# Attention scores, softmax and the turning of weights, one query block at a time instead of two

## The chip, the cores and the metric

The kernel runs on one core of a Trainium2 chip. The metric is the device time of one execution in microseconds (us). Engines are named as in the profile: PE (TensorE, matmuls and transposes), DVE (VectorE), ACT (ScalarE), POOL (GpSimd), SP (SyncE, which issues the weight loads).

## What is computed

A two-layer decoder trunk on 512 tokens of width 1024, all in float32: attention, gated MLP, short convolution, gated MLP. The change lies in the attention of the first layer. It has 16 heads of 64: eight forgetting heads (a softmax with a decay added to the scores) and eight stick-breaking heads.

```python
def forgetting_attention(q, k, v, log_f):      # heads 0..7, per block of 128 queries
    logits = einsum('bhqd,bhkd->bhqk', qi, k) * scale
    logits = logits + fi[..., :, None] - cum_f[:, :, None, :]
    logits = where(key_pos <= q_pos, logits, -inf)
    return einsum('bhqk,bhkd->bhqd', softmax(logits), v)

def stick_breaking_attention(q, k, v):         # heads 8..15
    z = einsum('bhqd,bhkd->bhqk', qi, k) * scale
    log_one_minus = where(key_pos < q_pos, log_sigmoid(-z), 0)
    later = reverse cumsum of log_one_minus over keys, without the own one
    w = where(key_pos < q_pos, exp(log_sigmoid(z) + later), 0)
    return einsum('bhqk,bhkd->bhqd', w, v)
```

Queries and keys are RMS-normed per head before. The heads' outputs go through one output projection and are added to the residual.

## The kernel before

Every float32 operand of a large matmul is split into two parts of fewer bits (hi and lo), and a product is three matmuls: hi by hi, hi by lo, lo by hi. Weights come by SP in pieces of 512 KB; ACT makes hi (L228) and DVE makes lo by a subtraction (L235), up to two pieces ahead.

Heads go in pairs p = 0..7 (0 to 3 forgetting, 4 to 7 stick-breaking), the two heads e of a pair on partitions 0 to 63 and 64 to 127. There are four blocks b of 128 queries; a "half" is two of them (0 and 1, or 2 and 3). For each pair and half:

- `logits(p, half)`, L537: the scores. Three matmuls per head and block (q hi by k hi, q hi by k lo, q lo by k hi; L552), a fourth for the decay of forgetting heads (L556), and a mask (L558). They contract over 64 rows, so the two heads of a pair lie side by side in the array. Each head and block has a PSUM bank "b" of its own, four per call, and there are four such banks. Forgetting heads then take the maximum on DVE (L569), the exponential on ACT (L571) and, later, the reciprocal and the scaling on DVE (L575, L576). Stick-breaking heads take two sigmoids on ACT (L582, L583), a backward product scan on DVE (L585) and a product on DVE (L586). The scores of block b reach over (b + 1) x 128 keys, at least 256.
- `turn(p, half)`, L591: the weights are transposed on PE (L604) into a bank "c" per head and block (there are two such banks), copied by ACT to hi (L606) and by DVE to lo (L609), which releases the bank. The tiles `pt` for them exist twice, for the two heads of one half. POOL zeroes the quarter that stays empty (L614).
- `weigh(p, half)`, L616: weights by values (L628, L629), 8 or 16 matmuls into a bank "a"; the two parts are added by ACT and DVE (L638, L639) and split (L316, L317).

Queries and keys come token-major from the input projection (`heads`), are normed per head there (a power on POOL at L313, then DVE at L510 and L513), and are transposed per pair by `turn_heads` (L530) with hi on ACT (L534) and lo on DVE (L535), two pairs at a time, into the same two banks "c".

What sets the order: the program is written with a planner's clock. `spend` advances it by an estimate for the PE work issued; `after(us, fn)` issues fn once the clock has passed; `fill(us)` issues work of the other kind for so many us: the input projections of the next head groups (L474 to L476, 256 columns) and, from the fourth pair on, half of the output projection (L250 to L252, L657). A tile scheduler then orders each engine's queue from it and may move instructions past each other. The main loop, u over 16 halves, issues `logits(u)`, FILL1, `weigh(u - 2)`, FILL1, `turn(u - 1)` (with FILL1 behind each of its two blocks) and FILL2 or, from u = 12, FILL3. When the fillers are used up, the rest of the output projection follows.

Of the kernel before, what the change touches and what calls it, by code (L numbers as in the profile page):

```python
# [25 lines left out]
P = 128  # L26
S = 512
# [12 lines left out]
SCALE, SHARES, LATER = 8.0, 1.5, 1.5  # L40
# [4 lines left out]
FILL1, FILL2, FILL3 = 1.0, 4.4, 2.6  # L45
# [3 lines left out]
def trunk(  # L49
# [21 lines left out]
    def f32(ap):  # L71
        return ap.bitcast(F32)
# [464 lines left out]
    def logits(p, half):  # L537
# [5 lines left out]
        both = [(b, e) for b in (2 * half, 2 * half + 1) for e in range(2)]  # L543
        ss = {be: bank("b") for be in both}

        def of(b, e):
            return slice(e * HD, (e + 1) * HD), slice(b * P, (b + 1) * P), slice(0, max((b + 1) * P, 256))

        for step, (ql, kl) in enumerate(((q_hi, k_hi), (q_hi, k_lo), (q_lo, k_hi))):
            for be in both:  # L550
                rows, tok, keys = of(*be)
                pe.matmul(ss[be][:, keys], ql[rows, tok], kl[rows, keys], start=step == 0, stop=False)  # L552
        if fox:
            for be in both:
                rows, tok, keys = of(*be)
                pe.matmul(ss[be][:, keys], dl[rows, p, tok], dr[rows, keys], start=False, stop=False)  # L556
        for be in both:
            pe.matmul(ss[be][:, of(*be)[1]], ident16, masks[0 if fox else 1], start=False, stop=True)  # L558
        spend((4 if fox else 3) * (0.4, 0.23)[half == 0] + 0.5)
        ws = {}  # L560
        tiles = [aw.tile([P, (3, 7)[half], P], F32, tag=f"w{half}", name=f"w{p}{half}{e}", bufs=2) for e in range(2)]
        for b, e in both:
            n = (b + 1) * P
            ws[b, e] = tiles[e].rearrange("p k c -> p (k c)")[:, (b % 2) * (n - P):][:, 0:n]
        if fox:
            tops, totals, invs = (
                {be: tiny.tile([P, 1], F32, tag=t, name=f"{t}{p}{be[0]}{be[1]}", bufs=8) for be in both} for t in ("top", "total", "inv"))
            for be in both:
                dve.reduce_max(tops[be], ss[be][:, 0:(be[0] + 1) * P], axis=AX.X, negate=True)  # L569
            for be in both:  # L570
                act.activation(ws[be], ss[be][:, 0:(be[0] + 1) * P], AF.Exp, bias=tops[be], accum_out=totals[be])  # L571

            def shares():
                for be in both:
                    dve.reciprocal(invs[be], totals[be])  # L575
                    dve.tensor_scalar(ws[be], ws[be], invs[be], None, op0=ALU.mult)  # L576
            after(SHARES, shares)
        else:
            for b, e in both:
                n, s, w = (b + 1) * P, ss[b, e], ws[b, e]  # L580
# [10 lines left out]
    def turn(p, half, ws):  # L591

        pts[p, half] = []
        for e in range(2):
            both = [aw.tile([P, NB, 256], F32R, tag=f"pt{i}", name=f"pt{p}{half}{e}{i}", bufs=PT) for i in range(2)]
            pts[p, half].append(both)
        for b in (2 * half, 2 * half + 1):
            n = (b + 1) * P
            at_ = slice((b % 2) * P, (b % 2 + 1) * P)
            srcs = []  # L600
            for e in range(2):
                t = bank("c")
                for k in range(b + 1):
                    pe.transpose(t[:, k * P:(k + 1) * P], ws[b, e][:, k * P:(k + 1) * P], ident)  # L604
                srcs.append(t[:, 0:n].rearrange("p (k q) -> p k q", q=P))
                act.activation(pts[p, half][e][0][:, 0:b + 1, at_], srcs[e], AF.Copy)  # L606
# [293 lines left out]
```

## Time and profile before

| | us |
|---|---|
| median of 3 runs | 1256.09 |
| lowest, highest | 1255.18, 1488.36 |
| the profiled execution | 1255.41 |
| span of its instructions | 1253.7 |

The profile lists, per engine, how long it was busy and what ended its idle time. Matmuls overlap in it: one of 256 columns shows 0.28 us, though the next starts 0.12 us later, so a busy PE need not be PE at its peak. The granted clock is 1.00 where PE runs at 2.4 GHz and 0.50 where it runs at 1.2. The attention stage with its loop lies between 72 and 306 us of the span; the two MLPs and the convolution follow.

### The profile page before, as it was taken

How to read it: one execution, taken by the hardware profiler on the slowest of the kernel's cores; microseconds unless marked ns; L12 is line 12 of the kernel's file. 1: busy time of each engine (PE TensorE's matmuls, PEld its weight loads, DVE VectorE, ACT ScalarE, POOL GpSimd, SP SyncE). 2: the span in 40 equal slices, each digit the busy share in tenths (PEclk: the TensorE clock that was granted, in tenths of full speed). 3: DMA queues.
4: the chain of work that ended last, by engine and by line, in shares of the span. 5: the costliest groups of instructions: out<-in, count | busy, mean ns of one | idle time of the engine just before them, and what ended most of it. 6: DMA issues, size and time to landing. Idle time of an engine off the chain costs nothing.

```text
span 1253.7 us, 15395 instructions
## 1 busy us (share of the span) xinstructions
PE 1212.9 (97%) x6133; PEld 1008.8 (80%) x6133; DVE 747.1 (60%) x1104; ACT 500.5 (40%) x815; POOL 49.6 (4%) x114
## 2 busy tenths in 40 slices
PE   7989999987999999999999999999999999999998
PEld 7978988766888888888888888888888888888886
DVE  4575677886676777765333455555667777772312
ACT  5454566554444344443222222233343444432120
POOL 3211111100000000000000000000000000000000
PEclk8998999997999999999999999999999999999999
DMA  5321221210323333333333323323233333332330
GB/s 157 93 61 34 69 62 40 68 51 18 100 85 101 95 91 101 88 93 93 93 93 97 101 85 100 99 87 100 85 101 96 89 101 89 96 101 84 104 115 34
DMA packets 175272, 108.15 MB, mean 86 GB/s; under 512 B 4604, under 2 KB 168492, under 8 KB 175200
## 3 DMA queue, kind: packets, MB, share of 16 engines
q1 hardware_dynamic: 174944, 107.01, 28.7%
q8 instruction: 48, 0.79, 0.3%
q0 software_dynamic: 256, 0.16, 0.1%
q14 instruction: 24, 0.20, 0.0%
HBM read 105.06 MB, written 2.10 MB: 85 GB/s over the span
## 4 chain that ended last, share of the span: by engine, by line
PE 87%; DVE 7%; ACT 3%; POOL 1%; DMA 1%; issue 1%; SPq 0%; DVEq 0%; ACTq 0%
PE psb L250 11%; PE psb L252 11%; PE psa L250 11%; PE psb L251 11%; PE psa L252 11%; PE psa L251 11%; PE psa L474 4%; PE psa L476 4%; PE psa L475 4%; PE psb L474 2%; PE psb L475 2%; PE psb L476 2%; DVE rest L585 2%; POOL qr L313 1%; PE psc L604 1%; PE psb L552 1%
## 5 line engine op out<-in xcount | busy, mean ns | idle before, releaser
L228 ACT ACTIVATE whi<-raw 128x1024 fp32r<-128x1024 f32 (+2 forms) x198 | 208.4, 1053 | 357.8 <-PE psb L251 131.1
L235 DVE TENSOR_TENSOR wlo<-raw,whi 128x1024 fp32r<-128x1024 f32 (+2 forms) x198 | 240.3, 1214 | 178.1 <-ACT whi L228 177.3
L250 PE MATMUL psb<-hs_hi,whi 128*128 128x512 f32 x480 | 189.9, 396 | 0.0
L252 PE MATMUL psb<-hs_hi,wlo 128*128 128x512 f32 x480 | 189.8, 395 | 0.0
L251 PE MATMUL psb<-hs_lo,whi 128*128 128x512 f32 x480 | 188.7, 393 | 0.0
L250 PE MATMUL psa<-hs_hi,whi 128*128 128x512 f32 x416 | 164.7, 396 | 0.0
L252 PE MATMUL psa<-hs_hi,wlo 128*128 128x512 f32 x416 | 164.2, 395 | 0.0
L251 PE MATMUL psa<-hs_lo,whi 128*128 128x512 f32 x416 | 163.9, 394 | 0.0
L324 DVE SCALAR_TENSOR_TENSOR u<-y,taps,u 128x510 f32<-128x510 f32 (+1 forms) x176 | 131.0, 747 | 3.0
L474 PE MATMUL psa<-whi,hs_hi 128*128 128x256 f32 (+1 forms) x384 | 114.0, 298 | 3.8 <-ACT sq L505 1.9
L476 PE MATMUL psa<-whi,hs_lo 128*128 128x256 f32 (+1 forms) x384 | 110.9, 289 | 0.0
L475 PE MATMUL psa<-wlo,hs_hi 128*128 128x256 f32 (+1 forms) x384 | 110.6, 288 | 0.0
L251 PEld LDWEIGHTS psb<-hs_lo,whi 128*128 128x128 f32 x480 | 90.1, 188 | 21.4
L252 PEld LDWEIGHTS psb<-hs_hi,wlo 128*128 128x128 f32 x480 | 90.1, 188 | 21.4
L250 PEld LDWEIGHTS psb<-hs_hi,whi 128*128 128x128 f32 x480 | 90.3, 188 | 20.3
L252 PEld LDWEIGHTS psa<-hs_hi,wlo 128*128 128x128 f32 x416 | 78.1, 188 | 18.6
L251 PEld LDWEIGHTS psa<-hs_lo,whi 128*128 128x128 f32 x416 | 78.1, 188 | 18.4
L250 PEld LDWEIGHTS psa<-hs_hi,whi 128*128 128x128 f32 x416 | 78.2, 188 | 18.0
L774 DVE TENSOR_TENSOR y<-psb,nrow_n 128x512 f32<-128x512 f32 x44 | 30.4, 691 | 83.9 <-PE psb L252 83.9
L474 PEld LDWEIGHTS psa<-whi,hs_hi 128*128 128x128 f32 x384 | 75.0, 196 | 5.0 <-ACT sq L505 2.2
L316 ACT ACTIVATE a<-u 128x512 fp32r<-128x512 f32 x44 | 27.8, 631 | 118.7 <-DVE u L779 118.7
L475 PEld LDWEIGHTS psa<-wlo,hs_hi 128*128 128x128 f32 x384 | 75.0, 195 | 0.0
(202 smaller groups left out, 1918.2 us busy)
## 6 DMA issues: line engine op xcount, KB each, us to landing
raw<-in_ffn_w_up SPq DMA_DIRECT2D x88, 512.0 KB, 3.8
raw<-in_ffn_w_down SPq DMA_DIRECT2D x30, 512.0 KB, 3.5
raw<-in_attn_w_in SPq DMA_DIRECT2D x24, 512.0 KB, 4.3
raw<-in_conv_w_in SPq DMA_DIRECT2D x24, 512.0 KB, 3.8
raw<-in_ffn_w_down SPq DMA_DIRECT2D x16, 448.0 KB, 3.6
raw<-in_attn_w_out SPq DMA_DIRECT2D x8, 512.0 KB, 3.4
raw<-in_conv_w_out SPq DMA_DIRECT2D x8, 512.0 KB, 4.0
x_tok<-in_x SPq DMA_DIRECT2D x4, 512.0 KB, 7.9
```

The costliest lines, as they stand in the source:

```text
L228: made = act.activation(hi[:, 0:nk * n], raw[:, 0:nk * n], AF.Copy)
L235: dve.tensor_tensor(lo[:, 0:nk * n], raw[:, 0:nk * n], f32(hi[:, 0:nk * n]), op=ALU.subtract)
L250: pe.matmul(acc, w[0], rhs[0], start=first, stop=False)
L251: pe.matmul(acc, w[0], rhs[1], start=False, stop=False)
L252: pe.matmul(acc, w[1], rhs[0], start=False, stop=last)
L316: act.activation(hi, src, AF.Copy)
L324: dve.scalar_tensor_tensor(dst[:, d:], src[:, 0:S - d], tap(j), dst[:, d:], op0=ALU.mult, op1=ALU.add)
L474: pe.matmul(acc, lhs[0], w[0], start=first, stop=False)
L475: pe.matmul(acc, lhs[0], w[1], start=False, stop=False)
L476: pe.matmul(acc, lhs[1], w[0], start=False, stop=last)
L585: dve.tensor_tensor_scan(back, back, back, 1.0, op0=ALU.mult, op1=ALU.bypass)
L774: dve.tensor_tensor(y, acc, norm.row, op=ALU.mult)
```

## The change

Scores, softmax and turning go by one query block instead of a half; weighing still goes by halves. The main loop runs over 32 blocks g: `logits(g)`, FILL1, `weigh` of the half of block g - 2 if that was the half's second, `turn(g - 1)`, FILL2 or FILL3. Each call of `logits` takes two banks "b" instead of four. The fillers' total stays nearly the same: 8.4 us per half before (FILL1 four times and FILL2) and 2 x (1.0 + 3.2) = 8.4 after; in the last two pairs 6.6 before and 2 x (1.0 + 2.0) = 6.0 after. The tiles for weights are four of 512 columns instead of two of 384 and two of 896; the small tiles for maxima and sums exist four times instead of eight; POOL's memsets are issued ahead of a half's first turn instead of behind its second. How queries and keys are made and kept token-major is not changed.

```diff
-SCALE, SHARES, LATER = 8.0, 1.5, 1.5
+SCALE, SHARES, LATER = 8.0, 1.0, 1.5
+WB = 4
-FILL1, FILL2, FILL3 = 1.0, 4.4, 2.6
+FILL1, FILL2, FILL3 = 1.0, 3.2, 2.0
...
-    def logits(p, half):
+    def logits(p, b):
...
-        both = [(b, e) for b in (2 * half, 2 * half + 1) for e in range(2)]
-        ss = {be: bank("b") for be in both}
+        n = (b + 1) * P
+        wide = max(n, 256)
+        tok = slice(b * P, n)
+        ss = [bank("b") for _ in range(2)]
         for step, (ql, kl) in enumerate(((q_hi, k_hi), (q_hi, k_lo), (q_lo, k_hi))):
-            for be in both:
-                rows, tok, keys = of(*be)
-                pe.matmul(ss[be][:, keys], ql[rows, tok], kl[rows, keys], start=step == 0, stop=False)
+            for e in range(2):
+                rows = slice(e * HD, (e + 1) * HD)
+                pe.matmul(ss[e][:, 0:wide], ql[rows, tok], kl[rows, 0:wide], start=step == 0, stop=False)
...
-        spend((4 if fox else 3) * (0.4, 0.23)[half == 0] + 0.5)
-        ws = {}
-        tiles = [aw.tile([P, (3, 7)[half], P], F32, tag=f"w{half}", name=f"w{p}{half}{e}", bufs=2) for e in range(2)]
+        spend((4 if fox else 3) * wide * 0.00044 + 0.12)
+        ws = [aw.tile([P, S], F32, tag="w", name=f"w{p}{b}{e}", bufs=WB)[:, 0:n] for e in range(2)]
...
-    def turn(p, half, ws):
+    def turn(p, b, ws):
+        half, n = b // 2, (b + 1) * P
+        if b % 2 == 0:
+            pts[p, half] = []
+            for e in range(2):
+                both = [aw.tile([P, NB, 256], F32R, tag=f"pt{i}", name=f"pt{p}{half}{e}{i}", bufs=PT) for i in range(2)]
+                for t in both:
+                    pool.memset(f32(t[:, 2 * half + 1, 0:P]), 0.0)
+                pts[p, half].append(both)
...
-            spend(0.22 * (b + 1))
-            fill(FILL1)
-        for both in pts[p, half]:
-            for t in both:
-                pool.memset(f32(t[:, 2 * half + 1, 0:P]), 0.0)
+        spend(0.22 * (b + 1))
...
-    for u in range(16 + 2):
-        p, half = divmod(u, 2)
-        if u < 16:
-            waiting[u] = logits(p, half)
-            if u % 4 == 3 and p < 7:
+    blocks = [(p, b) for p in range(8) for b in range(NB)]
+    for g in range(len(blocks) + 2):
+        if g < len(blocks):
+            p, b = blocks[g]
+            waiting[g] = logits(p, b)
+            if p % 2 and p < 7 and b == 3:
                 turn_heads(p + 1)
                 turn_heads(p + 2)
             fill(FILL1)
-        if u >= 2:
-            weigh(*divmod(u - 2, 2))
-            if u - 2 == 7:
+        if g >= 2 and blocks[g - 2][1] % 2:
+            p, b = blocks[g - 2]
+            weigh(p, b // 2)
+            if (p, b) == (3, 3):
                 fillers.append(output(0, residual))
-        if 1 <= u <= 16:
-            fill(FILL1)
-            turn(*divmod(u - 1, 2), waiting.pop(u - 1))
-            fill(FILL2 if u < 12 else FILL3)
+        if 1 <= g <= len(blocks):
+            turn(*blocks[g - 1], waiting.pop(g - 1))
+            fill(FILL2 if g < 24 else FILL3)
```

Line numbers after are one higher than before ahead of `logits` (L250 becomes L251) and lower from there on (L552 becomes L551, L585 becomes L578, L604 becomes L599, L609 becomes L604, L628 becomes L619).

On PE, the scores of the last pair's first half (blocks 0 and 1) before: four banks (psb_3490 to psb_3493) are filled step by step, and the scheduler has put fillers (L250 to L252, output projection) into the run.

```order
L552 MATMUL psb_3490<-qk_hi_3076,qk_hi_3085 128x256
L552 MATMUL psb_3491<-qk_hi_3076,qk_hi_3085 128x256
L552 MATMUL psb_3492<-qk_hi_3076,qk_hi_3085 128x256
L552 MATMUL psb_3493<-qk_hi_3076,qk_hi_3085 128x256
L552 MATMUL psb_3490<-qk_lo_3077,qk_hi_3085 128x256
L552 MATMUL psb_3491<-qk_lo_3077,qk_hi_3085 128x256
L552 MATMUL psb_3492<-qk_lo_3077,qk_hi_3085 128x256
L552 MATMUL psb_3493<-qk_lo_3077,qk_hi_3085 128x256
L552 MATMUL psb_3490<-qk_hi_3076,qk_lo_3086 128x256
L552 MATMUL psb_3491<-qk_hi_3076,qk_lo_3086 128x256
L250 MATMUL psa_3463<-o_hi_300,whi_3195 128x512
```

The same place after, block 0 of that pair: two banks (psb_3530, psb_3531), the row ahead of them a filler.

```order
L253 MATMUL psa_3516<-o_hi_300,wlo_3256 128x512
L551 MATMUL psb_3530<-qk_hi_3165,qk_hi_3174 128x256
L551 MATMUL psb_3531<-qk_hi_3165,qk_hi_3174 128x256
L551 MATMUL psb_3530<-qk_lo_3166,qk_hi_3174 128x256
L551 MATMUL psb_3531<-qk_lo_3166,qk_hi_3174 128x256
L551 MATMUL psb_3530<-qk_hi_3165,qk_lo_3175 128x256
L551 MATMUL psb_3531<-qk_hi_3165,qk_lo_3175 128x256
```

Where one run filled four banks, two runs now fill two each, with other PE work between them: counted over the program, 28 runs of score matmuls stand on PE before and 44 after.

On DVE, the end of the attention before: the scan and product of the last pair's block 3 (rest_3639, rest_3644, w_3627, w_3628), and behind them the subtractions of that pair's first half (pt_3674, pt_3676).

```order
L586 TENSOR_TENSOR w_3628<-w_3628,rest_3634 128x383
L585 SCALAR_TENSOR_TENSOR rest_3639<-rest_3639 128x511
L639 TENSOR_TENSOR o_3666<-psa_3649,o_3666 64x256
L586 TENSOR_TENSOR w_3627<-w_3627,rest_3639 128x511
L585 SCALAR_TENSOR_TENSOR rest_3644<-rest_3644 128x511
L639 TENSOR_TENSOR o_3666<-psa_3649,o_3666 64x256
L586 TENSOR_TENSOR w_3628<-w_3628,rest_3644 128x511
L317 TENSOR_TENSOR o_lo_2868<-o_3666,o_hi_2867 128x256
L609 TENSOR_TENSOR pt_3674<-psc_3677,pt_3673 128x128
L609 TENSOR_TENSOR pt_3676<-psc_3680,pt_3675 128x128
```

The same place after: a weight split (L236), the scans and products of block 3, and behind them the subtractions of block 2 (pt_3748, pt_3752).

```order
L236 TENSOR_TENSOR wlo_3808<-raw_3806,whi_3807 128x1024
L578 SCALAR_TENSOR_TENSOR rest_3721<-rest_3721 128x511
L578 SCALAR_TENSOR_TENSOR rest_3726<-rest_3726 128x511
L579 TENSOR_TENSOR w_3719<-w_3719,rest_3721 128x511
L579 TENSOR_TENSOR w_3720<-w_3720,rest_3726 128x511
L630 TENSOR_TENSOR o_3740<-psa_3731,o_3740 64x256
L604 TENSOR_TENSOR pt_3748<-psc_3755,pt_3747 128x3x128
L630 TENSOR_TENSOR o_3740<-psa_3731,o_3740 64x256
L604 TENSOR_TENSOR pt_3752<-psc_3760,pt_3751 128x3x128
```

Before, the subtractions of blocks 0 and 1 stand behind the scans and products of blocks 2 and 3; after, those of blocks 0 and 1 have moved ahead of the scans of block 3, and those of block 2 stand behind its scans and products.

On PE, the end of the attention before: two rows of the weighing of the pair before the last, the turns of the last pair's block 0 (one transpose per head) and block 1 (two per head), and the next weighing.

```order
L628 MATMUL psa_3649<-pt_3560,v_2974 128x256
L629 MATMUL psa_3649<-pt_3561,v_2974 128x256
L604 MATMUL psc_3677<-ident,w_3511 128x128
L604 MATMUL psc_3680<-ident,w_3512 128x128
L604 MATMUL psc_3685<-ident,w_3511 128x128 x2
L604 MATMUL psc_3689<-ident,w_3512 128x128 x2
L628 MATMUL psa_3699<-pt_3673,v_2974 128x256
```

After, the end of the last pair's first weighing, then the turns of block 2 (three transposes per head) and block 3 (four), and the last weighing.

```order
L619 MATMUL psa_3731<-pt_3644,v_3036 128x256
L620 MATMUL psa_3731<-pt_3645,v_3036 128x256
L599 MATMUL psc_3755<-ident,w_3677 128x128 x3
L599 MATMUL psc_3760<-ident,w_3678 128x128 x3
L599 MATMUL psc_3767<-ident,w_3719 128x128 x4
L599 MATMUL psc_3773<-ident,w_3720 128x128 x4
L619 MATMUL psa_3781<-pt_3747,v_3036 128x256
```

In both, two turns stand one behind the other on PE with nothing between them, the second in the same two banks "c" as the first; before these are blocks 0 and 1 (and further back 2 and 3), after only blocks 2 and 3.

## Rows read from the trace of the kernel before

**Rows 1.** The page's head and its section 1: busy time and share of the span.
```profile
span 1253.7 us, 15395 instructions
PE 1212.9 (97%) x6133; PEld 1008.8 (80%) x6133; DVE 747.1 (60%) x1104; ACT 500.5 (40%) x815; POOL 49.6 (4%) x114
```

**Rows 2.** Stretches: us, busy PE, PEld, DVE, ACT, POOL, granted clock, DMA share, GB/s.
```profile
91.10:97.90 6.80, 5.79 (x27) 5.79 (x28) 3.65 (x12) 3.20 (x8) 0.00 (x0) 0.50 0.00 0
115.00:118.30 3.30, 3.30 (x17) 3.22 (x17) 1.71 (x3) 0.69 (x1) 0.35 (x2) 0.50 0.00 0
289.10:302.60 13.50, 8.42 (x32) 6.92 (x33) 8.86 (x18) 5.67 (x14) 0.82 (x4) 0.50 0.00 0
72.00:306.00 234.00, 207.46 (x1561) 185.75 (x1560) 172.31 (x368) 132.41 (x329) 28.69 (x66) 0.95 0.17 50
185.00:306.00 121.00, 103.36 (x720) 88.88 (x718) 92.70 (x170) 69.13 (x164) 12.30 (x38) 0.94 0.17 53
```

**Rows 3.** Waits of PE, 72 to 306 us: us in total, times, longest.
```profile
PE psc L604 <- DVE pt L609: 9.1, 5, 6.7
PE psc L530 <- DVE qk_lo L535: 4.8, 3, 2.0
PE psa L250 <- DVE o L639: 2.9, 2, 1.8
PE psb L552 <- ACT w L571: 1.9, 2, 1.5
PE psa L474 <- ACT sq L505: 1.9, 1, 1.9
...
PE psb L552 <- ACT w L583: 0.9, 1, 0.9
...
PE psa L628 <- ACT sq L505: 0.5, 1, 0.5
```

**Rows 4.** Timeline of PE around a long score run: start us, us, instruction, count.
```profile
258.23 0.39 PE L251 MATMUL psa<-o_lo,whi 128*128 128x512 f32 x1
258.46 0.39 PE L252 MATMUL psa<-o_hi,wlo 128*128 128x512 f32 x1
258.77 0.68 PE L552 MATMUL psb<-qk_hi,qk_hi 64*128 64x384 f32 x4
...
260.20 0.40 PE L558 MATMUL psb<-mask,ident 128*128 128x128 bf16 x4
260.40 0.48 PE L250 MATMUL psa<-o_hi,whi 128*128 128x512 f32 x1
```

**Rows 5.** Timeline of PE around a short score run.
```profile
273.02 0.39 PE L252 MATMUL psa<-o_hi,wlo 128*128 128x512 f32 x1
273.33 0.39 PE L552 MATMUL psb<-qk_hi,qk_lo 64*128 64x256 f32 x2
273.65 0.40 PE L558 MATMUL psb<-mask,ident 128*128 128x128 bf16 x4
273.86 0.48 PE L250 MATMUL psa<-o_hi,whi 128*128 128x512 f32 x1
```

**Rows 6.** Timeline of PE, 89 to 93 us; in brackets the idle time before.
```profile
89.77 0.44 PE L552 MATMUL psb<-qk_hi,qk_hi 64*128 64x384 f32 x1 [1.49 <-ACT w L571]
92.11 0.58 PE L474 MATMUL psa<-whi,hs_hi 128*128 128x256 f32 x1 [1.91 <-ACT sq L505]
```

**Rows 7.** Waits of PE, 284 to 306 us.
```profile
PE psc L604 <- DVE pt L609: 7.4, 2, 6.7
```

**Rows 8.** Groups of DVE by line and shape, 74 to 305 us: busy, mean ns, idle before.
```profile
L235 DVE TENSOR_TENSOR wlo<-raw,whi 128x1024 fp32r<-128x1024 f32 x22 | 26.9, 1222 | 12.4 <-ACT whi L228 12.3
L585 DVE TENSOR_TENSOR_SCAN rest<-rest 128x511 f32<-128x511 f32 x8 | 9.6, 1211 | 0.0
L609 DVE TENSOR_TENSOR pt<-psc,pt 128x384 fp32r<-128x384 f32 x16 | 8.7, 553 | 0.8 <-ACT pt L606 0.6
L586 DVE TENSOR_TENSOR w<-w,rest 128x511 f32<-128x511 f32 x8 | 5.4, 682 | 0.2
```

More of the change, by code (lines that the diff above doesn't have):

```diff
@@ L553, in logits @@
         if fox:
[L554 to L558, printed above, removed]
-        spend((4 if fox else 3) * (0.4, 0.23)[half == 0] + 0.5)
-        ws = {}
-        tiles = [aw.tile([P, (3, 7)[half], P], F32, tag=f"w{half}", name=f"w{p}{half}{e}", bufs=2) for e in range(2)]
@@ L562, in logits @@
-        for b, e in both:
-            n = (b + 1) * P
-            ws[b, e] = tiles[e].rearrange("p k c -> p (k c)")[:, (b % 2) * (n - P):][:, 0:n]
-        if fox:
[L566 to L571, printed above, removed]
+            for e in range(2):
+                rows = slice(e * HD, (e + 1) * HD)
+                pe.matmul(ss[e][:, 0:wide], dl[rows, p, tok], dr[rows, 0:wide], start=False, stop=False)
@@ new lines, in logits @@
+        for e in range(2):
+            pe.matmul(ss[e][:, tok], ident16, masks[0 if fox else 1], start=False, stop=True)
+        spend((4 if fox else 3) * wide * 0.00044 + 0.12)
+        ws = [aw.tile([P, S], F32, tag="w", name=f"w{p}{b}{e}", bufs=WB)[:, 0:n] for e in range(2)]
+        if fox:
+            tops, totals, invs = ([tiny.tile([P, 1], F32, tag=t, name=f"{t}{p}{b}{e}") for e in range(2)] for t in ("top", "total", "inv"))
+            for e in range(2):
+                dve.reduce_max(tops[e], ss[e][:, 0:n], axis=AX.X, negate=True)
+            for e in range(2):
+                act.activation(ws[e], ss[e][:, 0:n], AF.Exp, bias=tops[e], accum_out=totals[e])
@@ L573, in shares @@
             def shares():
-                for be in both:
-                    dve.reciprocal(invs[be], totals[be])
-                    dve.tensor_scalar(ws[be], ws[be], invs[be], None, op0=ALU.mult)
+                for e in range(2):
+                    dve.reciprocal(invs[e], totals[e])
+                    dve.tensor_scalar(ws[e], ws[e], invs[e], None, op0=ALU.mult)
             after(SHARES, shares)
         else:
-            for b, e in both:
-                n, s, w = (b + 1) * P, ss[b, e], ws[b, e]
+            for s, w, e in zip(ss, ws, range(2)):
```

29 lines of the change are left out of this document (11 added, 18 removed).

## The prediction

> **What bounds the kernel now.** The page comes first: TensorE (PE) is busy for 97% of the span, VectorE (DVE) for 60% [rows 1]. That share is an average over stages, so the table of stretches comes next. Outside the attention stage PE runs without a gap; the stage that the change touches is the stretch from 72 to 306 us, where PE is busy for 207.5 of 234 us at a mean granted clock of 0.95 [rows 2]. Third, the waits of PE in that stretch: eleven rows, 26.0 us in all, the largest for DVE's subtraction that finishes the turned weights, 9.1 us, of which one wait alone is 6.7 [rows 3]. Three pieces of the stretch ran at half the granted clock, that is at 1.2 instead of 2.4 GHz: 5.8, 3.3 and 8.4 us of PE work stood in them [rows 2]; at full clock that work takes half, so they cost (5.8 + 3.3 + 8.4) / 2 = 8.8 us. Waits and clock together are 34.8 us. That is the most that a better order of this stage can give: neither kernel issues more or fewer instructions than the other (6121 matmuls, 1106 DVE and 781 ScalarE instructions in both orders), with the same shapes, and the DMA queue's order is the same.
>
> DVE is the second thing to see. From 185 to 306 us, mostly the stick-breaking heads, it is busy for 92.7 of 121 us while PE is busy for 103.4 [rows 2]. The two take turns waiting for each other there; neither is full.
>
> The sums below are made against the profiled execution, 1255.4 us with a span of 1253.7. The median of the runs shown is 1256.1, so a forecast is 0.7 us higher against it; I leave that out.
>
> **Term 1, more runs of score matmuls: +6.1 us.** The score matmuls use 64 rows of the array, everything around them 128. A run of 16 of them (12 of 64 rows, 4 masks) stands between the matmuls at 258.46 and 260.40. Matmuls of 512 columns follow each other at 0.23 us (258.23, 258.46), so the run took 1.94 - 0.23 = 1.71 us [rows 4]. Its columns at 2.4 GHz, with the two heads of a pair side by side, are three times (384 + 512) and four masks of 128: 3200 / 2.4 = 1.33 us. The rest, 0.38 us, is paid at the run's ends. A short run of 6 took 0.84 - 0.23 = 0.61 us for 768 columns, 0.32 us: rest 0.29 [rows 5]. So the price hangs on the run and hardly on its length. In PE's order there are 28 such runs before and 44 after (some are cut by the scheduler in both). 16 x 0.38 = 6.1 us. Bounds: 16 x 0.29 = 4.6, and 16 x 0.61 = 9.8 if each new run cost as much as a whole short one. Nothing hides this, since it is PE's own time.
>
> The Trainium skill, page TensorEngine Tiling (Array Packing), section Tiling Modes (Key Properties), says that changing the tiling mode, and not just the tile, drains TensorE. By that rule the sum counts mode changes, which gives the 6.1 us above; if instead the 0.3 to 0.4 us belonged to the matmuls themselves, whose number does not change, this term would be nothing and the forecast 6 us lower. Two runs of very different length with nearly the same rest speak for the rule.
>
> **Term 2, scores waiting for their banks: -5 us.** A call of logits takes all four "b" banks before and two after, so the next block's scores no longer need the exponentials of the block just issued to be done. The waits that this removes are 1.9 (for L571) and 0.9 us (for L583) [rows 3]. The first stands at 89.77 as 1.49 us, with a wait of 1.91 us for ScalarE right behind it at 92.11 [rows 6]: 3.4 us in which PE did almost nothing, and then the clock was at half for 6.8 us, worth 5.8 / 2 = 2.9 us [rows 2]. In all 1.9 + 0.9 + 1.9 + 2.9 = 7.6; I take 5, since ScalarE's square in that chain still sits in the same queue. Bounds 0 and -7.6.
>
> **Term 3, turned weights, except the last: -1.7 us.** Two turns of one call stood FILL1 = 1.0 us apart, and the second needs the two "c" banks that DVE's subtraction of the first releases. Now FILL2 = 3.2, a call of logits and FILL1 stand between them, over 5 us. Of the 9.1 us [rows 3] 7.4 are in the tail [rows 7]; the other 1.7 goes. Bounds 0 and -1.7.
>
> **Term 4, turning queries and keys: -2 us.** PE waits 4.8 us in three places for DVE (L535) [rows 3]. In the new order eight of these transposes stand directly behind a run that fills two score banks; before, four stood behind a run that filled four. So DVE has half the maxima and scalings ahead of them. I take 2 of the 4.8, and no change of the short stretch at half clock at 115 us [rows 2]. Bounds +2 and -4.8.
>
> **Term 5, output and value matmuls waiting: -3 us.** The other waits, from 2.9 for DVE (L639) down to 0.5 [rows 3], come from DVE's queue: in it four scans and four products stand as one block of work, two and two now. The six waits of this sort (all eleven but L604, L530, the two of L552 and the square of term 2) are 26.0 - 9.1 - 4.8 - 2.8 - 1.9 = 7.4 us; I take 3. Bounds 0 and -7.4.
>
> **Term 6, the tail: -1.1 us.** At the end of the stage the fillers are used up, and one of PE's two waits for DVE there is 6.7 us [rows 7]. The new order has the same knot: the last turn (four transposes per head) needs the "c" banks of block 2, and in DVE's queue the subtractions that release them stand behind a weight split and both scans and both products of block 3. With DVE's times that is 1.22 + 2 x 1.21 + 2 x 0.68 + 0.55 = 5.6 us [rows 8]. 6.7 - 5.6 = 1.1 less; the stretch at half clock that goes with it stays. Bounds 0 and -6.7, the latter if PE's own work covered it, plus 4.2 us of clock (8.4 / 2).
>
> The moved memsets cost nothing: ScalarE waits in both orders for the memset of the round before, and PE's next weighing comes 5 us later. SP's queue is not moved.
>
> **Sum.** 6.1 - 5 - 1.7 - 2 - 3 - 1.1 = -6.7, and 1255.4 - 6.7 = 1248.7, say 1249 us. That is 0.5%, inside the 2% (25 us) that a measurement of this kernel can tell from no change.
>
> **Rivals.**
> *The waits dissolve.* With smaller blocks PE and DVE overlap and the pieces at half clock go with the gaps. For it: DVE was free for 28 us of the 121 [rows 2], so there is room. Against it: the order of the tail keeps its knot. All of it would be 6.1 - 34.8 = -28.7, 1227 us; with the tail left (7.4 and 4.2 us of clock) it is -17.1, 1238. I give the middle of it, 1233.
> *The waits only move.* The work is the same, PE waits for DVE in other places, and the 16 runs are what is left: 1255.4 + 6.1 = 1261.5. For it: DVE's total is unchanged and near PE's.
> *The weights of a stick-breaking block come too late (slower).* Between the scores of block 3 and its turn the planner now puts FILL1, weighing (0.88), a turn (0.66), FILL2 or FILL3, the next scores (0.46) and FILL1: 7.2 us, and in the last two head pairs 6.0. Before, FILL1 six times and FILL2 stood there, 10.4 us, with a weighing or two, a turn and the next scores besides. DVE needs 2 x (1.21 + 0.68) for the block, and ahead of it 1.22 for a weight split and 2 x 0.55 for the turned block before, 6.1 us [rows 8], without ScalarE and the outputs. The point: as soon as these add 1 us, each of the eight large blocks (2 and 3 of four pairs) is late by about 1 us: +8, and if three of the gaps bring a stretch at half clock like that at 91 us, +8.7. With 6.1 for the runs and term 2 kept (-5): 1255.4 + 17.8 = 1273. Against it: the planner's fillers are costed near their real time, and DVE was only 77% busy.
> That the change does nothing can be left out: PE's order differs for 230 us.
>
> **How the numbers follow.** My forecast 0.50 (1240 to 1256), waits only moved 0.20 (1257 to 1266), waits dissolve 0.20 (1226 to 1240), late weights 0.10 (1267 to 1285). Range for 8 in 10: 1231 to 1270, which leaves out the ends of the second and last rivals. Faster by over 2% means below 1231: 0.07, from the dissolving waits alone; slower by over 2%, above 1281: 0.05; between them 0.88.
>
> **What would show it.** Right: runs of score matmuls that still lose 0.3 to 0.4 us each, PE's waits for L571 and L583 near nothing, a wait of 5 to 6 us at the last turn with a half clock after it, and the sum of PE's waits in the stage 12 to 16 us smaller. Wrong: runs that cost nothing (then lower by 6), waits for DVE spread over the blocks of the last four pairs (the slow rival), or a tail without a gap (the fast one).

## The result and the profile after

| | median us (runs) | ratio to before, 95% interval |
|---|---|---|
| before | 1254.99 (6) | |
| after | 1260.74 (6) | 1.0049 [1.0035, 1.0063] |

One of the six executions before took 1488.36 us; it is left out of the ratio, and the median of the other five is 1254.79. The changed kernel is 5.75 us slower; 1249, so 6.7 us less than the profiled execution before, was forecast. By the bound of 2% it is no change, but the interval leaves out both no difference and the forecast. The profiled execution after took 1260.63 us. The page's head and section 1 answer to [rows 1]:

```profile
span 1258.9 us, 15403 instructions
PE 1218.0 (97%) x6133; PEld 1008.7 (80%) x6133; DVE 746.8 (59%) x1104; ACT 499.8 (40%) x815; POOL 50.7 (4%) x114
```

The span is 5.2 us longer, PE is busy for 5.1 us more, and DVE's total is the same. So PE has more busy time, though the number of its instructions is unchanged. Next come the stretches of the attention stage (which now ends at 311 us), to be held against [rows 2]; the seventh column is the granted clock:

```profile
152.20:155.70 3.50, 3.50 (x20) 3.05 (x19) 0.57 (x4) 0.00 (x0) 0.00 (x0) 0.51 0.00 0
169.30:172.70 3.40, 2.91 (x14) 2.94 (x15) 1.17 (x3) 0.79 (x2) 0.00 (x0) 0.50 0.00 0
217.10:223.90 6.80, 4.61 (x20) 4.32 (x21) 4.43 (x11) 2.01 (x8) 0.00 (x0) 0.50 0.00 0
237.60:244.40 6.80, 6.29 (x28) 5.77 (x29) 4.89 (x10) 2.83 (x7) 0.00 (x0) 0.50 0.00 0
302.40:309.30 6.90, 6.07 (x25) 5.41 (x26) 3.45 (x7) 1.99 (x4) 0.00 (x0) 0.51 0.00 0
72.00:311.00 239.00, 213.68 (x1569) 187.80 (x1567) 172.45 (x368) 131.53 (x330) 29.73 (x66) 0.94 0.17 49
```

The three stretches at half clock of before are gone, except that of the tail, and four stand in new places: 3.5 + 2.9 + 4.6 + 6.3 + 6.1 = 23.4 us of PE work ran at 1.2 GHz instead of 17.5. Half of that is the cost: 11.7 against 8.8, 2.9 us more. Then PE's waits from 72 to 312 us, to be held against [rows 3], without the three smallest rows (1.0 us together):

```profile
PE psc L599 <- DVE pt L604: 9.2, 4, 4.7
PE psa L475 <- DVE o L630: 9.0, 3, 3.2
PE psa L475 <- DVE v L469: 2.7, 1, 2.7
PE psa L475 <- ACT sq L506: 1.4, 2, 0.9
PE psc L531 <- DVE qk_lo L536: 1.3, 1, 1.3
PE psc L599 <- DVE w L570: 0.8, 1, 0.8
...
```

All nine rows add up to 25.4 us, against 26.0 before. The waits for score banks (L552 before, L551 now) are gone, as forecast, and the turning of queries and keys waits 1.3 instead of 4.8. But there are four new stalls of about 3 us: a filler, the input projection (L475), waits for a bank "a" that DVE's addition of a weighing (L630) or a copy of values (L469) releases. The waits have moved.

Where they come from is to be read from the chain of waits, here the part in front of the first new stall, at 103 to 106 us (start us, us, what):

```profile
99.59 0.10 DVE qv L519
...
99.75 2.91 POOL qr L314
...
102.69 0.19 DVE qr L511
...
104.84 0.32 DVE o L630
105.16 0.40 DVE pt L604 x2
105.56 0.40 DVE v L469
...
106.00 0.39 PE psa L475
```

POOL's power (the exponent -0.5 by which queries or keys are normed; 2.9 us here) is followed in DVE's queue by the scaling that needs it (L511). An addition, a subtraction and a copy of other work stand behind it in the same queue, and PE waits for the copy. The next sight of it is the timeline of DVE in front of the fourth new stall:

```profile
233.41 0.17 DVE L519 TENSOR_SCALAR qv<-qv 128x16 f32<-128x16 f32 x1
...
233.89 0.40 DVE L630 TENSOR_TENSOR o<-psa,o 64x256 f32<-64x256 f32 x1
236.60 0.17 DVE L511 TENSOR_TENSOR qr<-qr,ncol_n 128x16 f32<-128x16 f32 x1 [2.31 <-POOL qr L314]
236.81 0.69 DVE L514 TENSOR_TENSOR qk<-qk,qr 128x512 f32<-128x512 f32 x1
237.53 0.43 DVE L630 TENSOR_TENSOR o<-psa,o 64x256 f32<-64x256 f32 x1
```

and that of PE at the same place:

```profile
234.60 0.34 PE L551 MATMUL psb<-qk_lo,qk_hi 64*128 64x384 f32 x2
238.11 0.55 PE L475 MATMUL psa<-whi,hs_hi 128*128 128x256 f32 x1 [3.17 <-DVE o L630]
```

One of the weighing's two additions stands ahead of the scaling, the other behind it; DVE is idle for 2.3 us, then scales for 0.9, and PE starts again 0.6 us after the second addition began, at half clock. The view of PE's waits names L630, and that hides the cause: the wait of DVE itself names it, in the waits of DVE from 72 to 312 us:

```profile
DVE qr L511 <- POOL qr L314: 12.1, 5, 3.0
```

The same view of the kernel before (72 to 306 us) had such a row at its top, and the prediction did not use it:

```profile
DVE qr L510 <- POOL qr L313: 13.8, 6, 3.0
```

### The profile page after: what moved, and what is told of

Its sections match the earlier page's. It is cut to its first block, busy times and chain, and to the rows that moved or that the text cites. A ratio compares the mean times of both kernels' runs of the same rounds, so it can differ in the third digit from the quotient of the medians.

```text
span 1258.9 us, 15403 instructions
## 1 busy us (share of the span) xinstructions
PE 1218.0 (97%) x6133; PEld 1008.7 (80%) x6133; DVE 746.8 (59%) x1104; ACT 499.8 (40%) x815; POOL 50.7 (4%) x114
## 4 chain that ended last, share of the span: by engine, by line
PE 88%; DVE 5%; ACT 3%; POOL 2%; issue 1%; DMA 1%; SPq 0%; DVEq 0%; ACTq 0%
PE psa L251 11%; PE psb L251 11%; PE psb L253 11%; PE psb L252 11%; PE psa L253 11%; PE psa L252 11%; PE psa L475 4%; PE psa L477 4%; PE psa L476 4%; PE psb L476 2%; PE psb L475 2%; PE psb L477 2%; POOL qr L314 2%; DVE wlo L236 1%; PE psc L599 1%; PE psb L551 1%
## 5 line engine op out<-in xcount | busy, mean ns | idle before, releaser
L236 DVE TENSOR_TENSOR wlo<-raw,whi 128x1024 fp32r<-128x1024 f32 (+2 forms) x198 | 240.2, 1213 | 173.2 <-ACT whi L229 172.2
L251 PE MATMUL psb<-hs_hi,whi 128*128 128x512 f32 x480 | 189.9, 396 | 0.0
L252 PE MATMUL psb<-hs_lo,whi 128*128 128x512 f32 x480 | 188.7, 393 | 0.0
L251 PE MATMUL psa<-hs_hi,whi 128*128 128x512 f32 x416 | 164.7, 396 | 0.0
L252 PE MATMUL psa<-hs_lo,whi 128*128 128x512 f32 x416 | 163.9, 394 | 0.0
L475 PE MATMUL psa<-whi,hs_hi 128*128 128x256 f32 (+1 forms) x384 | 116.8, 305 | 14.0 <-DVE o L630 9.0
L252 PEld LDWEIGHTS psb<-hs_lo,whi 128*128 128x128 f32 x480 | 90.1, 188 | 21.4
L251 PEld LDWEIGHTS psb<-hs_hi,whi 128*128 128x128 f32 x480 | 90.3, 188 | 20.3
L252 PEld LDWEIGHTS psa<-hs_lo,whi 128*128 128x128 f32 x416 | 78.1, 188 | 18.4
L251 PEld LDWEIGHTS psa<-hs_hi,whi 128*128 128x128 f32 x416 | 78.2, 188 | 18.0
L475 PEld LDWEIGHTS psa<-whi,hs_hi 128*128 128x128 f32 x384 | 76.1, 199 | 16.7 <-issue 10.2
L477 PEld LDWEIGHTS psa<-whi,hs_lo 128*128 128x128 f32 x384 | 76.0, 198 | 0.0
```

The costliest lines, as they stand in the source:

```text
L236: dve.tensor_tensor(lo[:, 0:nk * n], raw[:, 0:nk * n], f32(hi[:, 0:nk * n]), op=ALU.subtract)
L251: pe.matmul(acc, w[0], rhs[0], start=first, stop=False)
L252: pe.matmul(acc, w[0], rhs[1], start=False, stop=False)
L475: pe.matmul(acc, lhs[0], w[0], start=first, stop=False)
L477: pe.matmul(acc, lhs[1], w[0], start=False, stop=last)
```

## The experiments

Theory A: the 16 further runs of score matmuls cost some 5 us, and the waits that the change removed came back because DVE stands in its queue for POOL's power. Rivals: B, DVE is simply full and the power only shows as the last to end; C, turning by one block costs the time by itself; and that the moved memsets do. Later two forms of A were told apart: A1, the power's wait costs as much before as after; A2, it became costly by the change. All ratios are to the kernel before, timed on the same chip each time; its medians were 1254.6 to 1255.1 us, so times of different experiments are held against each other below. Line numbers shift by a few lines with each edit.

**Runs of score matmuls cut in two, in the kernel before.** The two blocks of each call get a run of their own, with a filler step between them:

```diff
-FILL1, FILL2, FILL3 = 1.0, 4.4, 2.6
+FILL1, FILL2, FILL3 = 1.0, 3.7, 1.9
...
+        for part in (both[:2], both[2:]):
             for step, (ql, kl) in enumerate(...):
-                for be in both:
+                for be in part:
...
+            if part[0][0] % 2 == 0:
+                fill(0.7)
```

> The kernel before, with each call's run of score matmuls cut in two by a filler step: 44 runs instead of 28, the same banks, turns and tiles. Theory A (each further run costs PE 0.32 us, as the 44 runs of the changed kernel show): 16 x 0.32 = 5.1, so 1260 us (1258 to 1262), and the runs lose 0.3 to 0.4 us each in the trace. Rival B (runs cost nothing, the 5.75 us of the change are waits): 1255, give or take 2.

1265.02 us, 1.0074 [1.0059, 1.0089]: 10.4 us more than before, twice the 5.1 of theory A; a miss for both. The 36 runs, or pieces of runs between fillers, that no wait cuts and that ran at full clock lose 0.33 us each up to their end (median, worked out as in term 1). The rest is clock: of its six executions the one with a mean granted clock of 0.989 took 1260.4 us and the one with 0.981, which is the profiled one, 1267.0. In that one 27.1 us of PE work of the stage ran at half clock, 9.6 us more than the 17.5 of before, which is 4.8 us. So the run is no clean price of the runs.

**The scaling later, in the changed kernel.** DVE's scaling of head groups 1 to 3 is issued behind the subtractions of the second turn that follows, and pinned there:

```diff
-        after(SCALE, scale)
+        if g:
+            pend.append([0, scale])
+        else:
+            after(SCALE, scale)
...
-            turn(*blocks[g - 1], waiting.pop(g - 1))
+            last = turn(*blocks[g - 1], waiting.pop(g - 1))
+            for item in list(pend):
+                item[0] += 1
+                if item[0] >= 2:
+                    pend.remove(item)
+                    item[1](last)
```

> The changed kernel, with DVE's scaling of queries and keys (the instructions behind POOL's power) put behind the subtractions of the second turn that follows, so DVE need not stand idle for POOL. Theory A (in the changed kernel DVE stands in its queue for the power, 12.1 us in 5 places, and PE's stalls of 2.9, 2.9, 3.2, 4.2 and 3.4 us and four stretches at half clock come from it): DVE's waits for POOL under 2 us, PE's waits in the stage down from 25.4 to 8 to 14 us, time 1240 to 1252. Rival B (DVE is simply full, and the power only shows as the last to end): other DVE work ends the same stalls, time 1258 to 1263.

1236.79 us, 0.9860 [0.9847, 0.9872]: 24 us less than the changed kernel, 18 less than before. DVE has no wait for POOL left in the stage, while its busy time is that of the changed kernel (172.8 us, 172.5 there), and PE's waits there (72 to 288 us) begin with

```profile
PE psc L607 <- DVE pt L612: 5.2, 3, 4.7
PE psa L476 <- ACT sq L509: 1.5, 2, 1.1
PE psc L539 <- DVE qk_lo L544: 1.3, 1, 1.3
PE psc L607 <- DVE w L578: 0.8, 1, 0.8
PE psa L476 <- DVE o L639: 0.7, 2, 0.4
```

Of the four new stalls of the filler nothing is left but 0.7 us for L639 (L630 there) and 0.4 for the values; only the tail keeps its 4.7. This kernel has the same 44 runs of score matmuls. Rival B falls.

**One half of the change at a time.** First the scores two blocks at a time as before, with turns by one block:

```diff
-            waiting[g] = logits(p, b)
+            if b % 2 == 0:
+                both = logits(p, b // 2)
+                for i in range(2):
+                    waiting[g + i] = [both[b + i, e] for e in range(2)]
```

> The changed kernel with one part undone: scores and softmax two query blocks at a time as before (32 runs), turning by one block as in the changed kernel. Theory A: 12 runs fewer x 0.32 = -3.8, so 1257, with the waits for score banks back (2 to 3 us) 1257 to 1260. Rival C (turning by one block is what costs): 1260 to 1264.

1252.22 us, 0.9979 [0.9971, 0.9988]: faster than both, which neither theory said. Then the other half, scores by one block and turns by two:

```diff
-            turn(*blocks[g - 1], waiting.pop(g - 1))
+            p, b = blocks[g - 1]
+            if b % 2:
+                turn(p, b // 2, {(b - i, e): waiting[g - 1 - i][e] for i in range(2) for e in range(2)})
```

> The changed kernel with the other part undone: scores and softmax by one block (47 runs), turning two blocks at a time as before. Theory A: 19 runs more than the kernel before x 0.32 = +6.1, so 1261 (1259 to 1266). Rival C (turning by one block is what costs): 1254 to 1257.

1261.92 us, 1.0060 [1.0048, 1.0072]. Here the memsets, FILL1 behind each turned block and six tiles for weights instead of four go with the turns by two. The four kernels make a square: scores by one block cost 7.3 us with long turns (1261.9 - 1254.6, the median of before in that sitting) and 8.5 with short ones (1260.7 - 1252.2, the changed kernel from its own sitting); turns by one block give back 2.4 and 1.2. Rival C falls: the scores are the part that costs. `SHARES` and the tiles for weights go with the scores in these runs and were not varied alone.

**The scaling later, in the kernel before.** The edit is that of the second run, with the count of turned blocks taken inside `turn`.

> The kernel before, with the scaling of queries and keys put behind the subtractions of the second turned block that follows, as in the run of the changed kernel with it (33 runs of score matmuls). In the kernel before DVE also stands for POOL's power, 13.8 us in 6 places. Theory A1 (the wait for the power costs PE in both kernels, and the change only moved where): the kernel before gains much of what the changed one gained (24 us), 1238 to 1248. Theory A2 (in the kernel before PE's stalls have other causes, the four score banks and the turns, and the power becomes costly only by the change): 1250 to 1257.

1250.83 us, 0.9966 [0.9955, 0.9977], 4 us less: it looked like A2. But this edit pins other work too: PE got a new wait of 4.0 us for a copy of values that now stands behind the scaling, one wait of DVE for POOL, 3.0 us, remains, and the scheduler made 33 runs of score matmuls out of the 28. So it did not settle the question.

**The power twice, in both kernels.** For head groups 1 to 3, the second time for nothing:

```diff
-        rsqrt(r.rearrange("p b h -> p (b h)"), total.rearrange("p b h -> p (b h)"))
+        for _ in range(2 if g else 1):
+            rsqrt(r.rearrange("p b h -> p (b h)"), total.rearrange("p b h -> p (b h)"))
```

> The changed kernel with POOL's power for head groups 1 to 3 issued twice, the second time for nothing: the suspected wait doubled (3.2 us more on POOL in six places, five of which show as a wait in DVE's queue). Theory A (DVE stands in its queue for the power, and PE for DVE): DVE's waits for POOL grow from 12.1 to 26 to 31 us, PE's waits behind them by about as much, 5 x 2.9 = 14.5 plus clock: 1272 to 1285. Rival B (the power only shows as the last to end): 1259 to 1265.

1281.34 us, 1.0202 [1.0178, 1.0226]: 20.6 more than the changed kernel, as theory A has it. DVE's wait for POOL (72 to 330 us) and PE's first three waits (72 to 333 us):

```profile
DVE qr L511 <- POOL qr L314: 29.5, 6, 6.0
```

```profile
PE psa L475 <- DVE o L631: 18.0, 3, 6.2
PE psc L600 <- DVE pt L605: 14.7, 4, 7.0
PE psa L475 <- DVE v L469: 5.7, 1, 5.7
```

Held against the rows of after, 9.0 in three waits has become 18.0 in three, and 2.7 has become 5.7: each new stall grew by 3.0 us, as long as one power. In the kernel before:

> The same doubling in the kernel before. Theory A2 (there the wait is mostly covered, since PE has whole halves of scores and turns ahead of what DVE holds up): as its removal gave 4 of 13.8 us, 17 us more of it cost about 5, 1257 to 1263. Theory A1 (as costly as in the changed kernel): 1267 to 1280.

1276.14 us, 1.0167 [1.0149, 1.0185]: 21.3 more, as A1 has it. DVE's wait for POOL grew from 13.8 us (its row above) to

```profile
DVE qr L510 <- POOL qr L313: 31.2, 6, 6.0
```

These 17.4 us are paid in full: in the profiled execution PE's waits grew by 13.4 us (26.0 to 39.4), and 28.6 instead of 17.5 us of its work ran at half clock, which is 5.6 more. What A2 has right is only that the first 13.8 are partly covered, as the run with the scaling on POOL then measured.

**The memsets as before.** In the changed kernel, the four memsets of a half are put back behind its second turn.

> The changed kernel with POOL's memsets of the turned tiles put back behind a half's second turn, as before. If moving them cost nothing: 1259 to 1262.5. If they held up POOL's power or ScalarE's copies: 1254 to 1258.

1261.67 us, 1.0056 [1.0037, 1.0074], the same as the changed kernel within the intervals. Moving them cost nothing that can be measured.

**The scaling on POOL, in both kernels.** POOL multiplies behind its own power, so nothing in DVE's queue waits for it, and nothing in that queue is pinned:

```diff
         def scale():
-            dve.tensor_tensor(r, r, norm.col[:, :, None].to_broadcast([P, NB, 4]), op=ALU.mult)
+            eng = pool if g else dve
+            eng.tensor_tensor(r, r, norm.col[:, :, None].to_broadcast([P, NB, 4]), op=ALU.mult)
...
-                dve.tensor_tensor(t, t, r[:, 2 * j:2 * j + 2, :, None].to_broadcast([P, 2, 4, HD]), op=ALU.mult)
+                eng.tensor_tensor(t, t, r[:, 2 * j:2 * j + 2, :, None].to_broadcast([P, 2, 4, HD]), op=ALU.mult)
```

> The changed kernel with the scaling of queries and keys done by POOL, behind its own power, for head groups 1 to 3: DVE has nothing in its queue that waits for POOL, by another way than moving it in DVE's queue. Theory A: DVE's waits for POOL near nothing, PE's four stalls behind them gone, 1238 to 1250 (POOL's multiplications of 128x512 are not in any trace yet; if they come late, the turning of queries and keys waits for POOL instead, at most 3 times). Rival B: 1258 to 1263.

The changed kernel with it: 1238.67 us, 0.9869 [0.9850, 0.9887], 22.1 less than the changed kernel. A second way of taking the wait out gives the same as the first. In the profiled executions PE's waits fell from 25.4 to 11.9 us and its work at half clock from 23.4 to 4.3, which makes 13.5 + 9.6 = 23.1; the spans differ by 21.7. The line's instructions, durations as min/median/max in ns, on POOL for groups 1 to 3 and on DVE for group 0:

```profile
L515 POOL TENSOR_TENSOR qk<-qk,qr x12: 1042/1044/1691, 84.2 to 222.4; 128x512 f32<-128x512 f32 x12
...
L515 DVE TENSOR_TENSOR qk<-qk,qr x4: 679/689/694, 40.3 to 52.7; 128x512 f32<-128x512 f32 x4
```

POOL takes 1.04 us where DVE takes 0.69, and the kernel is 22 us faster by it. The Trainium skill, page GPSIMD Engine Reference, section Engine selection, gives elementwise work to VectorE, with GpSimd about twice as slow for two inputs. The trace has 1.5 times here. In this kernel the choice by duration would have been the wrong one: what counted was the queue that the instruction blocks while it waits.

> The kernel before with the scaling of queries and keys on POOL, as in the run of the changed kernel with it (which fell by 22 us): nothing in DVE's queue waits for POOL, and nothing else in that queue is pinned. Theory A2 (in the kernel before the wait for the power is mostly covered or stands beside other waits): 1248 to 1253. Theory A1 (it costs there nearly what it costs in the changed kernel, and the run with the scaling moved later lost that again by what it moved): 1234 to 1243.

The kernel before with it: 1246.60 us, 0.9930 [0.9917, 0.9944], 8.5 less than before, between A1 and A2. Of PE's waits that are left (72 to 297 us) the largest, those at the turning of queries and keys (L531) and those for exponentials (L572, L571 before):

```profile
PE psc L605 <- DVE pt L610: 9.2, 5, 6.7
...
PE psc L531 <- POOL qk L514: 1.1, 1, 1.1
...
PE psc L531 <- DVE qk_lo L536: 0.9, 1, 0.9
...
PE psb L553 <- ACT w L572: 0.5, 1, 0.5
```

Of the 4.8 us at the turning of queries and keys 2.0 are left, 1.1 of them for POOL's multiplication, of the 1.9 us for exponentials 0.5, and the stretches at half clock at 91 and 115 us are gone (the one at the end of the stage is left, with 8.4 us of PE work):

```profile
91.10:97.90 6.80, 6.80 (x59) 6.36 (x58) 4.43 (x7) 3.92 (x7) 0.07 (x1) 1.00 0.15 26
115.00:118.30 3.30, 3.30 (x37) 3.03 (x36) 1.71 (x4) 0.94 (x4) 0.00 (x0) 1.00 0.71 178
```

So in the kernel before the power stood behind most of the waits that terms 2 and 4 laid to score banks and to DVE's load; the smaller wait for a bank, 0.9 us for L583, is still there. The run also takes the multiplications, twelve of 0.69 us, off DVE; in the changed kernel the run with the scaling later shows that this is not what helps, in the kernel before no run parts the two. The timeline of DVE before shows it in front of the stall of [rows 6]: the maxima (L569) on which that block's exponentials wait stand behind the scaling, and its inputs behind 3.0 us of POOL.

```profile
84.88 0.17 DVE L518 TENSOR_SCALAR qv<-qv 128x16 f32<-128x16 f32 x1
88.06 0.18 DVE L510 TENSOR_TENSOR qr<-qr,ncol_n 128x16 f32<-128x16 f32 x1 [3.01 <-POOL qr L313]
...
88.88 1.15 DVE L569 TENSOR_REDUCE top<-psb 128x1 f32<-128x128 f32 x4
```

**The price of the runs once more.** The cut runs of the first experiment together with the scaling on POOL:

> The kernel before with scaling on POOL and each run of score matmuls cut in two (44 runs): against the run without the cut, the price of 16 runs where fewer stalls and stretches at half clock blur it. If a run costs 0.33 us: 5.3 more than that run (4 to 7). If the 10 us of the first run with cut runs were the price of the runs themselves: 9 to 11 more.

1250.02 us, 0.9960 [0.9948, 0.9973], 3.4 more than without the cut, under the expected 4 to 7; the two intervals, some 1.6 us to either side each, leave 1 to 6, so the 10 us of the first run are not the price of the runs. In the profiled executions some 1.5 us of the difference are clock (11.3 instead of 8.4 us at half clock). By the rows it is 3.9: 44 runs at 0.33 are 14.5 us, 28 at 0.38 (the median of 21 such ones before) are 10.6.

**Other orders with the wait gone.** Scores two blocks at a time, turns by one, scaling later:

> Scores two blocks at a time (35 runs), turning by one block, and the scaling later. If the runs and the wait for the power are separate causes that add: 1252.2 - (1260.7 - 1236.8) x (the power's stalls here, 2.9 + 2.9 + 2.6 of 12.4) = 1236, at best 1233 with 9 runs fewer x 0.33. Rival (short scores are needed once the power's wait is gone, since long ones hold all four score banks): 1239 to 1246.

1239.63 us, 0.9885 [0.9869, 0.9902], where its rival had it: 2.8 slower than with short scores. With the power's wait in the queue long scores were 8.5 us faster, without it they are slower, though they have 9 runs fewer. The tail, the end of the stage, was tried in three kernels by one number, FILL3 from 2.0 to 1.4, so that output matmuls are left between the last two turns:

> The changed kernel with the scaling later, and FILL3 1.4 instead of 2.0, so that twelve matmuls of the output projection are left between the turns of the last two blocks. If the wait at the last turn (4.7 us) and the stretch at half clock behind it (6.8 us, 5.1 of PE work in it, worth 2.6) are what is left of the tail: 4.7 + 2.6 less minus what the smaller FILL3 opens elsewhere, 1230 to 1235. Rival: the wait moves to the blocks that get fewer fillers, 1236 to 1240.

> The same with FILL3 1.4, nine output matmuls between the last two turns: 3 to 6 us less than without, if the tail is a cause of its own; the same time if its wait only moves.

> The changed kernel with scaling on POOL and FILL3 1.4: the tail's wait of 4.7 us and its half clock covered by output matmuls. By the run with the scaling later (1236.8, with FILL3 1.4 1234.3) 2 to 3 us less than 1238.7: 1235 to 1237; 1232 if POOL's scaling leaves DVE room there.

With the scaling later 1234.31 us, 0.9843 [0.9828, 0.9857], 2.5 less, which by the intervals is hardly clear of nothing; with long scores 1240.27, no less (a wait of 3.1 us near the end and 5.2 us of PE work at half clock are left); with the scaling on POOL 1235.14, 0.9839 [0.9826, 0.9852], 3.5 less. The first of them has no stretch at half clock left in its stage, which ends at 285 us:

```profile
72.00:285.00 213.00, 203.47 (x1564) 177.59 (x1563) 172.57 (x368) 131.21 (x330) 30.66 (x66) 1.00 0.18 54
```

The first and the last of these beat the kernel before by 20 us and the changed one by 26: the order of the change, FILL3 1.4, and the scaling behind later turns or on POOL.

## Why the prediction was wrong

What happened is the rival "the waits only move": 1261.5 was its time, and PE's waits are 25.4 instead of 26.0 us, with DVE as their last cause in other places. It gave the equality of DVE's totals as its reason; that was not the cause. That its time came within 1 us is partly luck: it had 6.1 us for the runs and nothing for the clock, and the clock cost 2.9, the runs less than 6.1 by most readings (term 1 below). The forecast's counts of instructions (6121, 1106, 781) are not those of the page, 6133, 1104 and 815; that they are equal in both kernels holds.

The table has us of PE's waits, from the rows shown: of the turned weights 9.1 - 6.7 before and 9.2 - 4.7 after; for term 5 what is left when the waits of the others are taken off, 25.4 - 9.2 - 1.3 - 1.4 = 13.5 after, and 10.9 - 5.2 - 1.3 - 1.5 = 2.9 with the scaling later (10.9 is the sum of its nine rows).

By these rows the difference of the profiled executions is 3.9 us for the runs of score matmuls, -0.6 for waits and 2.9 for the clock, 6.2 together; the spans differ by 5.2.

| step | forecast, us | in the changed kernel | with the scaling later in it |
|---|---|---|---|
| term 1, runs | +6.1 | +3.9 by rows (+3.4 as timed in the old order, scaling on POOL) | the same 44 runs |
| term 2, score banks | -5 | waits 2.8 to 0, ScalarE's square (L505) 1.9 to 1.4; clock in the whole stage +2.9 | |
| term 3, turned weights except the longest wait | -1.7 | 2.4 to 4.5, +2.1 | 0.5 left |
| term 4, queries and keys | -2 | 4.8 to 1.3, -3.5 | 1.3 |
| term 5, output and values | -3 | 7.4 to 13.5, +6.1 | 2.9 left |
| term 6, tail | -1.1 | 6.7 to 4.7, -2.0 | 4.7 |

**Term 1** had the right mechanism; how far its price was too high is open. It charged the 16 new runs 0.38 each, but cutting also makes the old ones cheaper, since a run of half the length loses 0.33 instead of 0.38. 3.9 by the rows and 3.4 as timed (1 to 6 by the intervals) lie below its lower bound of 4.6, and the 5.2 us between the spans leave 2.9 for the runs. But these rows end where the run ends: the matmul behind it loses some 0.09 us more, as the one behind a mask alone does (last section), and for 16 runs that would be 1.4. By these readings the term is off by 1 to 3 us; terms 3 and 5 are off by 13 (-4.7 forecast, +8.2 measured).

**Term 2** came true for the waits, and its cause was misread. It laid the 3.4 us at 90 us and the half clock behind them to banks that are released late. With the scaling on POOL the old order, with the same four banks, has neither: these banks were late because the power was. Only the 0.9 us for L583 stay there, and the new order is rid of them.

**Term 4** came out better than taken, for the same reason: what the turning of queries and keys waited for was DVE's queue behind the power (2.0 of 4.8 us are left when it is out, in the old order).

**Terms 3 and 5** are the steps that failed. Term 5 took DVE's queue as work that comes in smaller pieces, term 3 the distance between two turns, and both bounded the new waits at nothing. In the new order the weighing's additions and the turns' subtractions stand behind the scaling, so PE's wait for them became as long as the power: four stalls of 2.7 to 3.2 us where term 5 forecast 4.4 us of waits in all, and one of the turns besides, 4.1 us at 214. None of the terms had new stretches at half clock behind new stalls either; with them the clock cost 2.9 us more, where term 2 had counted on up to 2.9 less. A bound of 13.8 us above nothing was to be had from the row of DVE's waits for POOL before. Without that wait, the last column, both terms hold.

**Term 6** is near its forecast: 4.7 us instead of 5.6, and the half clock behind it stayed. That its cover would take the clock's loss away too is shown by the two kernels with short scores and FILL3 1.4, which have no stretch at half clock in the stage.

**The sum.** Taking the scaling out of DVE's queue is worth 8.5 us in the kernel before and 22.1 in the changed one, so the change raised the price of the power's wait by 13.5 us; the intervals leave 10 to 17. In the profiled executions PE's waits fell by 6.4 us before (26.0 to 19.6) and by 13.5 after, the cost of the clock by 4.6 and by 9.6. With the scaling on POOL in both, the change makes the kernel 7.9 us faster (1246.60 to 1238.67); -6.7 was forecast. So the error of the forecast is mainly that one interaction; that -7.9 comes so near to -6.7 is in part luck, since the causes of terms 2 and 4 were others. Of the list of what would show it, the runs, the two waits near nothing and, nearly, the tail (4.7 us for 5 to 6) were right, and the sum of PE's waits, 12 to 16 us smaller, was wrong.

Of the other rivals, "the waits dissolve" is what happens once the wait is out (1234 to 1239 us; 1233 was given). "Weights of a stick-breaking block come too late" did not happen: its waits would have been for L578 and L579, and PE's rows name them nowhere. Why the same wait costs 13.5 us more in the new order is shown by the rows at two of its places, not for each; the rest is inferred from the stalls that vanish with it.

## What to carry to other kernels

A wait of an engine that is "not the bottleneck" is to be followed to what stands behind it in the same queue: before moving work on PE, list every instruction of the engines that PE waits for which itself waits for a third one, and price what now comes behind it. PE's own view names the last in the queue (an addition), and only DVE's view names the cause. Such an instruction is best moved behind work that is ready, or onto the engine that it waits for, even where that engine is slower at it; then try the order again, since the sign of its effect may turn.

## What the runs showed of the hardware

POOL's power costs more with more columns: 3.2 us on average for 128x16 (25.3 us for 8), 1.0 for 128x4 in the same trace; no other width was run. The first of these is longer than DVE's scan over 511 columns [rows 8].

```profile
L314 POOL TENSOR_TENSOR qr<-qv,minus_half 128x16 f32<-128x16 f32 x8 | 25.3, 3167 | 75.3 <-DVE qv L519 75.3
...
L314 POOL TENSOR_TENSOR ncol_n<-nv_n,minus_half 128x4 f32<-128x4 f32 x4 | 4.1, 1016 | 597.5 <-DVE nv_n L283 597.5
```

Most of what a run of score matmuls loses belongs to its 64-row matmuls. In the first experiment the scheduler left a mask alone (all 128 rows) between fillers; the timeline of PE:

```profile
258.13 0.40 PE L252 MATMUL psa<-o_hi,wlo 128*128 128x512 f32 x1
258.37 0.23 PE L559 MATMUL psb<-mask,ident 128*128 128x128 bf16 x1
258.41 0.48 PE L250 MATMUL psa<-o_hi,whi 128*128 128x512 f32 x1
258.73 0.39 PE L251 MATMUL psa<-o_lo,whi 128*128 128x512 f32 x1
```

From 258.13 to 258.73 are 0.60 us, two matmuls of 512 columns (0.23 each) and a mask of 128 columns (0.05): 0.09 lost, all of it behind the mask (0.32 us from 258.41 to the next matmul instead of 0.23), where runs with 64-row matmuls lose 0.33 up to their end alone. The Trainium skill, page TensorEngine Tiling (Array Packing), section Tiling Modes, under Key Properties, says that a change of the tiling mode drains TensorE. The trace agrees as far as it goes, since the mask changes no mode and loses less; the drain itself is not in a row.

Each of the five stretches at half clock in the changed kernel's stage begins within one of PE's stalls of 2.7 to 4.7 us or 1.0 us behind it; the sixth such stall, at 103 us, was followed by none. In the run with the memsets as before the same stall (2.7 us) was followed by 3.4 us at half clock. Between executions of one kernel the mean granted clock differs, and the time with it: 6.5 us lay between two executions of the kernel with cut runs, whose clocks were 0.989 and 0.981.
